# Strassen's seven products for two thirds of the matrix products of a hybrid decoder layer

## The chip, the cores and the metric

The kernel runs on one core of one Trainium2 chip. Its time is the device time of one execution in microseconds (us). The core has a matrix engine (TensorE, PE in the profile, with a unit PEld that loads the stationary operand), a vector engine (DVE), a scalar engine (ACT), GpSimd (POOL) and an engine that here only issues DMAs (SyncE, SP). Each engine works through its own list of instructions in a fixed order; semaphores make one wait for another.

## The reference

A layer for 1024 tokens of width 2048 in float32. One input projection of the normalised input feeds two recurrences: mLSTM with four heads (query, key, value, output gate, z gate, two scalar gates) and HGRN2 with eight heads (query, forget gate, value, output gate). Both are gated, joined, projected back and added to the input; a per-layer input and a second gate follow.

```python
u = rmsnorm(h, norm_w[l])
proj = jnp.einsum('bsd,dc->bsc', u, w_in[l])           # 2048 -> 8200 columns
(ml_q, ml_k, ml_v, ml_o, ml_z, ml_i, ml_f, hg_q, hg_f, hg_i, hg_g) = jnp.split(proj, ...)
h_a = mlstm_chunkwise(q_a, k_a, v_a, i_pre, f_pre)     # q_a, k_a: convolution and silu of ml_q, ml_k
y_a = sigmoid(ml_o) * rmsnorm(h_a) * silu(ml_z)
h_b = hgrn2_chunkwise(q_b, k_b, logf_b, i_b)
y_b = rmsnorm(h_b) * silu(hg_g)
h = h + jnp.einsum('bsc,cd->bsd', concat(y_a, y_b), w_out[l])
e = jnp.einsum('bsr,rd->bsd', p[l], w_pe[l])
gate = sigmoid(jnp.einsum('bsd,de->bse', rmsnorm(h, pe_norm_w[l]), w_pg[l]))
out = rmsnorm(h + gate * e, final_norm_w)
```

## The kernel before

Tokens are handled in two halves of 512. Every large product is a float32 product made of three float32r matmuls: each operand is the sum of a rounded part (hi) and an exact remainder (lo), and `mm3` (lines 241 to 244) issues hi·hi, hi·lo and lo·hi into one accumulator. Making the two parts of an operand is a `split` (lines 113 to 115): a cast on ACT, then a subtraction on DVE.

Weights stream through SBUF in slices of 128 x 1024, each used once per half: `next_piece` (line 140) issues the DMA on SP and the split, three slices ahead of their use (`AHEAD`), into three raw and three split buffers. A block is 256 columns, four slices. `proj_ch` (line 246) puts channels on the output partitions: 96 matmuls of 512 columns into two PSUM banks. `proj_tok` (line 258) puts tokens there: 192 matmuls of 256 columns into four banks. Per half there are 32 blocks: each mLSTM head takes query with key, output gate, values and z; each pair of HGRN2 heads takes values, two blocks of query with forget gate, and the output gate.

The recurrences (`mlstm_unit`, line 342; `hgrn_unit`, line 464) are written behind their own projections. They are chains of small steps that go back and forth between DVE, ACT and PE in chunks of 128 tokens. An mLSTM head multiplies scores (`psc`, `pkt`), then runs over four chunks with a state C (`pn`, `pu`), then a norm (`rh`) and transposes (`pth`). A pair of HGRN2 heads sums elementwise products (`cs_`), doubles block sizes five times (`pl`), updates a state (`hkt`, `hpu`) and reads it out (`hpo`, `hpt`). A tile scheduler decides each engine's order when the kernel is built; it lays these steps between the projection matmuls of later blocks.

The second part (from line 662) does for each half the output projection (`po`, 4 blocks of 512 columns, 8 slices each) with the residual and transposes of the result (`pht`, `hnt`, kept in SBUF), then in `gate_block` the per-layer input (`pe`) and the gate (`pg`), then the final norm. Half 0's output projection is free to start while half 1's recurrences still run.

Matmuls of 512 columns, or as much: 4608 `pj`, 3072 of 256 columns `pt` (1536 as counted in 512), 1536 `po`, 1536 `pg`, 192 `pe`.

Of the kernel before, what the change touches and what calls it, by code (L numbers as in the profile page):

```python
# [869 lines left out]
```

## Time and profile before

| | us |
|---|---|
| median of 3 runs (2429.05 to 2429.24) | 2429.08 |
| span of the profiled execution | 2427.2 |
| PE busy | 2410.4 (99%) |
| PEld busy (beside PE) | 2044.1 (84%) |
| DVE busy | 1166.3 (48%) |
| ACT busy | 767.8 (32%) |
| POOL busy | 66.3 (3%) |
| DMA moved 287.57 MB, mean | 118 GB/s |

The profiled execution's own time is its span and the little around it: the median of the runs is 1.9 us over the span. A group's busy time counts where instructions overlap only once for the engine, but a matmul's own "mean ns" includes the filling of the pipeline, so two neighbours overlap; the step from one start to the next (the pitch) is read from the timeline.

### The profile page before, as it was taken

To read this page: it belongs to the slowest core of one execution; us is meant where nothing else is said; L and a number is where in the kernel's file an instruction comes from. 1 tells how busy PE (TensorE), PEld (TensorE's weight loads), DVE (VectorE), ACT (ScalarE), POOL (GpSimd) and SP (SyncE) were. 2 spreads that over 40 slices of the span, in tenths; PEclk is the share of its full clock that TensorE was granted. 3 is DMA by queue.
4 is the path that set the end of the run, shared out by engine and by line. 5 is a ranking of instruction groups with operands and counts; after the bars stand their busy time and mean duration, and the time that the engine had idled before them with its cause. 6 is when DMAs were issued, how large, how long until landed. Compare 5 with 4: busy or idle time off the path is not lost.

```text
span 2427.2 us, 30855 instructions
## 1 busy us (share of the span) xinstructions
PE 2410.4 (99%) x12700; PEld 2044.1 (84%) x12700; DVE 1166.3 (48%) x1657; ACT 767.8 (32%) x1211; POOL 66.3 (3%) x96
## 2 busy tenths in 40 slices
PE   8999999999999999999999999999999999999998
PEld 7888889888888888888888888888888888888887
DVE  6655344355564847344246364565423444332336
ACT  6433232223222424223222222242322334332225
POOL 0000000000000000000000000000000000000000
PEclk9999999999999999999999999999999999999999
DMA  8433332222222423333332222243444446444336
GB/s 315 136 97 103 94 100 94 91 78 93 79 87 81 156 78 105 96 108 101 94 107 87 87 79 89 78 150 122 135 130 127 132 146 222 135 154 130 117 114 212
DMA packets 93461, 287.57 MB, mean 118 GB/s; under 512 B 10872, under 2 KB 11640, under 8 KB 93320
## 3 DMA queue, kind: packets, MB, share of 16 engines
q1 hardware_dynamic: 88200, 268.82, 35.0%
q0 software_dynamic: 5120, 16.78, 1.8%
q8 instruction: 99, 1.62, 0.3%
q14 instruction: 42, 0.34, 0.0%
HBM read 260.36 MB, written 25.20 MB: 118 GB/s over the span
## 4 chain that ended last, share of the span: by engine, by line
PE 98%; DMA 0%; issue 0%; DVE 0%; ACT 0%; SPq 0%; POOL 0%; POOLq 0%; ACTq 0%; DVEq 0%
PE pj L244 15%; PE pj L243 15%; PE pj L242 15%; PE pg L242 5%; PE pt L242 5%; PE pg L244 5%; PE pt L244 5%; PE pg L243 5%; PE po L242 5%; PE pt L243 5%; PE po L244 5%; PE po L243 5%; PE pl L570 2%; PE pe L242 1%; PE pe L244 1%; PE pe L243 1%
## 5 line engine op out<-in xcount | busy, mean ns | idle before, releaser
L242 PE MATMUL pj<-u,hl 128*128 128x512 f32 x1536 | 608.0, 399 | 5.9 <-ACT hl L114 5.9
L244 PE MATMUL pj<-u,hl 128*128 128x512 f32 x1536 | 611.3, 399 | 0.0
L243 PE MATMUL pj<-u,hl 128*128 128x512 f32 x1536 | 610.8, 398 | 0.2 <-DVE u L230 0.2
L114 ACT CAST hl<-raw 128x1024 fp32r<-128x1024 f32 (+2 forms) x259 | 269.2, 1040 | 863.1 <-PE pj L244 449.1
L115 DVE TENSOR_TENSOR hl<-raw,hl 128x1024 fp32r<-128x1024 f32 (+2 forms) x259 | 313.5, 1211 | 402.4 <-ACT hl L114 402.2
L242 PEld LDWEIGHTS pj<-u,hl 128*128 128x128 f32 x1536 | 289.1, 188 | 72.6 <-ACT hl L114 5.9
L243 PEld LDWEIGHTS pj<-u,hl 128*128 128x128 f32 x1536 | 289.4, 188 | 70.0 <-DVE u L230 1.1
L244 PEld LDWEIGHTS pj<-u,hl 128*128 128x128 f32 x1536 | 289.1, 188 | 66.7 <-issue 0.2
L242 PE MATMUL pt<-hl,u 128*128 128x256 f32 (+1 forms) x1024 | 291.1, 285 | 0.4 <-DVE raw L357 0.4
L244 PE MATMUL pt<-hl,u 128*128 128x256 f32 (+1 forms) x1024 | 290.2, 285 | 0.0
L243 PE MATMUL pt<-hl,u 128*128 128x256 f32 (+1 forms) x1024 | 288.8, 283 | 0.0
L242 PE MATMUL po<-hl_o,ys 128*128 128x512 f32 x512 | 202.1, 395 | 0.0
L244 PE MATMUL po<-hl_o,ys 128*128 128x512 f32 x512 | 200.3, 392 | 0.0
L243 PE MATMUL po<-hl_o,ys 128*128 128x512 f32 x512 | 199.8, 390 | 0.0
L242 PEld LDWEIGHTS pt<-hl,u 128*128 128x128 f32 x1024 | 193.7, 189 | 2.2 <-issue 1.1
L243 PEld LDWEIGHTS pt<-hl,u 128*128 128x128 f32 x1024 | 194.0, 189 | 1.3
L244 PEld LDWEIGHTS pt<-hl,u 128*128 128x128 f32 x1024 | 192.4, 188 | 0.9 <-issue 0.2
L242 PE MATMUL pg<-hl_g,hnt 128*128 128x512 f32 x448 | 177.9, 397 | 0.0
L244 PE MATMUL pg<-hl_g,hnt 128*128 128x512 f32 x448 | 177.9, 397 | 0.0
L243 PE MATMUL pg<-hl_g,hnt 128*128 128x512 f32 x448 | 177.1, 395 | 0.0
L115 DVE TENSOR_TENSOR hl_o<-raw_o,hl_o 128x1024 fp32r<-128x1024 f32 x64 | 78.4, 1225 | 161.9 <-ACT hl_o L114 161.9
L115 DVE TENSOR_TENSOR hl_g<-raw_g,hl_g 128x1024 fp32r<-128x1024 f32 x56 | 68.6, 1225 | 174.5 <-ACT hl_g L114 174.5
(264 smaller groups left out, 2642.9 us busy)
## 6 DMA issues: line engine op xcount, KB each, us to landing
raw<-in_w_blk_dram SPq DMA_DIRECT2D x247, 512.0 KB, 3.9
raw_o<-in_w_out_dram SPq DMA_DIRECT2D x64, 512.0 KB, 3.6
...
yr<-y SPq DMA_DIRECT2D x32, 256.0 KB, 4.0
xr<-in_x_dram SPq DMA_DIRECT2D x32, 256.0 KB, 5.7
h<-ht POOLq DMA_DIRECT2D x32, 256.0 KB, 6.3
hr<-h SPq DMA_DIRECT2D x32, 256.0 KB, 3.6
out_dram<-h SPq DMA_DIRECT2D x32, 256.0 KB, 3.5
```

Source lines behind the costliest of these rows:

```text
L114: nc.scalar.copy(out=dst_hi, in_=src)
L115: nc.vector.tensor_tensor(out=dst_lo, in0=src, in1=dst_hi.bitcast(F32), op=ALU.subtract)
L242: nc.tensor.matmul(ps, lhsT=ah, rhs=bh, start=first, stop=False)
L243: nc.tensor.matmul(ps, lhsT=ah, rhs=bl, start=False, stop=False)
L244: nc.tensor.matmul(ps, lhsT=al, rhs=bh, start=False, stop=last)
L570: nc.tensor.matmul(pl[0:M, c * 64:(c + 1) * 64], lhsT=kf[:, c * P:c * P + M], rhs=qv[:, c * nb:(c + 1) * nb, 1, :], start=True, stop=True)
```

## The change

Seven products in place of eight (Strassen's scheme in Winograd's form). A group takes 512 tokens, 2048 input channels and 1024 columns, cut into quarters: two of 256 tokens, two of 1024 channels, two of 512 columns. Four sums of quarters of the tokens' operand (S1 to S4) and four sums of quarters of the weights stand in the seven products P1 to P7, and the products are added up into the four quarters of the output. It is used for values, all gates of the input projection (5 groups per half), the output projection (2 groups per half) and the second gate of half 0 (2 groups): 16 groups. Query, key and forget-gate projections stay as they were, with channels on partitions; so does the second gate of half 1, with tokens on partitions.

A product has 4 slices of weights of 128 x 1024 and 12 matmuls of 512 columns per slice, so a group has 28 slices and 336 matmuls.

The program is cut into stages that hand over through DRAM.

- Stage a: all of the per-layer input first (192 matmuls `pe`, stored to DRAM), `prep_u` (the norm of the input is now applied to the input, and u is stored to DRAM), then ten groups; gates and values go to DRAM with their nonlinearities applied.
- Stage b: u is loaded and split again; projections of 12 blocks per half, and the recurrences, in the order HGRN2 pair 0, mLSTM head 0, pair 1, head 1 and so on, gates and values loaded from DRAM. The mLSTM scalar gates have 64 matmuls of their own (`pif`).
- Stage c: four groups of the output projection, the residual, transposes stored to DRAM; then half 0's normalised hidden state through DRAM, two groups, and half 1's second gate as before.

All seven operands of the tokens are made in `aprep` before a set of groups: 28 splits and 16 sums of 128 x 512.

```diff
-    upool = ctx.enter_context(tc.tile_pool(name="upool", bufs=17))
-    wpool = ctx.enter_context(tc.tile_pool(name="wpool", bufs=3))
+PRODUCTS = ("P1", "P5", "P2", "P6", "P3", "P7", "P4")
+A_SETS = ("A11", "S1", "A12", "S2", "S4", "S3", "A22")
+    class Gemm:
+            self.up = pool(f"up{tag}", self.st, bufs=28)
+            self.r1p = pool(f"rp{tag}", self.st, bufs=4, side="right")
+            self.hlp = pool(f"hp{tag}", self.st, bufs=3, side="right")
+            self.stp = pool(f"sp{tag}", self.st, bufs=5, side="right")
...
+        def t2(self, name):
+            return self.tp.tile([P, HT], F32, tag="t2", bufs=9, name=name)
...
+                if prod == "P1":
+                    raw = self.r1p.tile([P, 1024], F32, tag="r1", name=f"r1_{n}")
+                    nc.sync.dma_start(out=raw, in_=q["B11"])
+                    self.chain[j] = raw
+                elif prod in ("P5", "P6", "P4"):
+                    raw = self.chain[j]
...
+                        t = self.load(f"s_{n}", b)
+                        nc.vector.tensor_tensor(out=raw, in0=raw, in1=t, op=ALU.add)
+                elif prod == "P7":
+                    raw = self.load(f"s_{n}", q["B12"])
+                    t = self.load(f"t_{n}", q["B22"])
+                    nc.vector.tensor_tensor(out=raw, in0=raw, in1=t, op=ALU.add)
+                else:
+                    raw = self.load(f"s_{n}", q["B21" if prod == "P2" else "B22"])
+            hl = self.hlp.tile([P, 2, 1024], F32R, tag="hl", name=f"hl_{n}")
+            split(hl[:, 0], hl[:, 1], raw)
...
+        for j in range(4):
+            a, b = ld(j + 4, 1), ld(j, 1)
+            c = t2v(f"c{nm}_{j}")
+            nc.vector.tensor_tensor(out=c, in0=a, in1=b, op=ALU.subtract)
+            sc.append(c)
+            put("S1", j, c)
...
+                if pr == "P1":
+                    nc.scalar.copy(out=t("p1", p, "p"), in_=X)
+                elif pr == "P5":
+                    nc.vector.tensor_tensor(out=t("p15", p, "q"), in0=X, in1=tmp["p1", p], op=ALU.add)
+                elif pr == "P2":
+                    done(p, 0, 0, X, None)
+                elif pr == "P6":
+                    nc.vector.tensor_tensor(out=t("u2", p, "r"), in0=X, in1=tmp["p1", p], op=ALU.add)
...
+    for k in range(KT):
+        t = G.t2(f"hk{k}")
+        nc.sync.dma_start(out=t, in_=hT_dram[0][k // 2][k % 2])
+        nc.vector.scalar_tensor_tensor(out=t, in0=t, scalar=vec_sb[:, V_PEN + k:V_PEN + k + 1], in1=rb,
+                                       op0=ALU.mult, op1=ALU.mult)
+        nc.gpsimd.dma_start(out=n_dram[k // 2][k % 2], in_=t)
+    A = aprep(G, "g0", n_dram)
...
+UNITS = [("h", 0), ("m", 0), ("h", 1), ("m", 1), ("h", 2), ("m", 2), ("h", 3), ("m", 3)]
```

The scheduler orders the new program anew. The first place is PE's order at an mLSTM head. Before, at head 1 of half 0, `pn0_1` (chunks read out) and `pu0_1` (state updates) of its recurrence, and `pj0_8`, the projection of a later block:

```order
L243 MATMUL pj0_8_1_1762<-u0_2_179,hl_0_8_0_1600 128x512
L244 MATMUL pj0_8_1_1762<-u0_2_179,hl_0_8_0_1600 128x512
L432 MATMUL pn0_1_1_1699<-C0_1_0_1690,dq0_1_1664 128x257 [waits DVE_49]
L430 MATMUL pn0_1_2_1713<-vt0_1_1531,dq0_1_1664 128x257
L242 MATMUL pj0_8_0_1761<-u0_3_182,hl_0_8_0_1600 128x512
L243 MATMUL pj0_8_0_1761<-u0_3_182,hl_0_8_0_1600 128x512
L244 MATMUL pj0_8_0_1761<-u0_3_182,hl_0_8_0_1600 128x512
L432 MATMUL pn0_1_2_1713<-C0_1_1_1704,dq0_1_1664 128x257 [waits DVE_49]
L435 MATMUL pu0_1_2_1716<-vt0_1_1531,kh0_1_1681 128x257
L242 MATMUL pj0_8_1_1762<-u0_3_182,hl_0_8_0_1600 128x512
L243 MATMUL pj0_8_1_1762<-u0_3_182,hl_0_8_0_1600 128x512
```

Now, for the same head. `pj0_10` is a projection block of the following pair of HGRN2 heads, `pth0_1` the head's last transposes:

```order
L96 MATMUL pj0_10_1_9087<-u0_15_6816,hl_0_10_3_9118 128x512
L642 MATMUL pn0_1_0_8282<-vt0_1_8233,dq0_1_8260 128x257 [waits DMAHW5_49,DVE_49,Activation_49]
L647 MATMUL pu0_1_0_8284<-vt0_1_8233,kh0_1_8277 128x257 [waits DVE_49,Activation_49]
L642 MATMUL pn0_1_1_8295<-vt0_1_8233,dq0_1_8260 128x257 [waits PE_49]
L647 MATMUL pu0_1_1_8298<-vt0_1_8233,kh0_1_8277 128x257 [waits PE_49]
L644 MATMUL pn0_1_1_8295<-C0_1_0_8286,dq0_1_8260 128x257 [waits DVE_49]
L642 MATMUL pn0_1_2_8309<-vt0_1_8233,dq0_1_8260 128x257
L644 MATMUL pn0_1_2_8309<-C0_1_1_8300,dq0_1_8260 128x257 [waits DVE_49]
L647 MATMUL pu0_1_2_8312<-vt0_1_8233,kh0_1_8277 128x257
L642 MATMUL pn0_1_3_8323<-vt0_1_8233,dq0_1_8260 128x257 [waits DVE_49,Activation_49]
L647 MATMUL pu0_1_3_8326<-vt0_1_8233,kh0_1_8277 128x257 [waits DVE_49,Activation_49]
L644 MATMUL pn0_1_3_8323<-C0_1_2_8314,dq0_1_8260 128x257 [waits DVE_49]
L669 MATMUL pth0_1_0_8344<-ident_62,h0_1_8280 128x128 [waits DVE_49]
```

Before, the chunks of the head are laid between projection matmuls; now none stands between the head's first chunk and its last transposes.

The second place is PE's order at the end of the recurrences. Before, near the end of the last pair of half 1 (`hkt1_3`, `hpu1_3`: keys transposed and state update), with the output projection of half 0 (`po0_1`):

```order
L242 MATMUL po0_1_3_13057<-hl_o0_1_0_12937,ys0_1_12675 128x512
L243 MATMUL po0_1_3_13057<-hl_o0_1_0_12937,ys0_1_12675 128x512
L244 MATMUL po0_1_3_13057<-hl_o0_1_0_12937,ys0_1_12675 128x512
L242 MATMUL po0_1_2_13056<-hl_o0_1_1_12966,ys0_2_12680 128x512
L601 MATMUL hpu1_3_0_12579<-hv1_3_12073,hkh1_3_12572 128x128 [waits Activation_49]
L601 MATMUL hpu1_3_0_12579<-hv1_3_12073,hkh1_3_12572 128x128 x3
L597 MATMUL hkt1_3_1_12590<-ident_86,kg1_3_12079 128x128 [waits PE_49]
L597 MATMUL hkt1_3_1_12590<-ident_86,kg1_3_12079 128x128 x3
L243 MATMUL po0_1_2_13056<-hl_o0_1_1_12966,ys0_2_12680 128x512
L244 MATMUL po0_1_2_13056<-hl_o0_1_1_12966,ys0_2_12680 128x512
L242 MATMUL po0_1_3_13057<-hl_o0_1_1_12966,ys0_2_12680 128x512
```

Now, at the end of the last mLSTM head of half 1 (`pn1_3`, `pth1_3`), and the first product of the output projection (`pso00`):

```order
L642 MATMUL pn1_3_3_12771<-vt1_3_12682,dq1_3_12707 128x257
L644 MATMUL pn1_3_3_12771<-C1_3_2_12762,dq1_3_12707 128x257 [waits DVE_49]
L669 MATMUL pth1_3_0_12788<-ident_62,h1_3_12727 128x128 [waits DVE_49,Activation_49]
L669 MATMUL pth1_3_1_12796<-ident_62,h1_3_12727 128x128
L669 MATMUL pth1_3_0_12788<-ident_62,h1_3_12727 128x128 [waits DVE_49]
L669 MATMUL pth1_3_1_12796<-ident_62,h1_3_12727 128x128
L669 MATMUL pth1_3_0_12788<-ident_62,h1_3_12727 128x128 [waits DVE_49]
L669 MATMUL pth1_3_1_12796<-ident_62,h1_3_12727 128x128
L669 MATMUL pth1_3_0_12788<-ident_62,h1_3_12727 128x128 [waits DVE_49]
L669 MATMUL pth1_3_1_12796<-ident_62,h1_3_12727 128x128
L94 MATMUL pso00_X0_1_13016<-hl_o0_0_P1_0_13020,A11o0_0_12837 128x512 [waits Activation_49]
L95 MATMUL pso00_X0_1_13016<-hl_o0_0_P1_0_13020,A11o0_0_12837 128x512 [waits DVE_49]
```

Before, the output projection fills the gaps of the last recurrences; now its first matmul stands behind the last transposes of the last head.

The third place is DVE's order in the output projection. Before, in half 0 (`hl_o`: remainders of weight slices; `hnt`: transposed result; `ht`: residual added):

```order
L115 TENSOR_TENSOR hl_o0_1_6_13175<-raw_o0_1_6_13174,hl_o0_1_6_13175 128x1024 [waits DMAHW6_49,Activation_49]
L115 TENSOR_TENSOR pp0_12748<-praw0_0_12749,pp0_12748 128x512 [waits Activation_49]
L115 TENSOR_TENSOR pp0_12748<-praw0_1_12753,pp0_12748 128x512 [waits Activation_49]
L709 SCALAR_TENSOR_TENSOR hnt0_0_13027<-pht0_0_13022,vec_sb_82,hnt0_0_13027 128x512 [waits Activation_49]
L709 SCALAR_TENSOR_TENSOR hnt0_1_13035<-pht0_1_13030,vec_sb_82,hnt0_1_13035 128x512 [waits Activation_49]
L709 SCALAR_TENSOR_TENSOR hnt0_2_13043<-pht0_2_13038,vec_sb_82,hnt0_2_13043 128x512 [waits DMASW3_49,DMASW2_49,Activation_49]
L709 SCALAR_TENSOR_TENSOR hnt0_3_13051<-pht0_3_13046,vec_sb_82,hnt0_3_13051 128x512 [waits Activation_49]
L115 TENSOR_TENSOR hl_o0_1_7_13204<-raw_o0_1_7_13203,hl_o0_1_7_13204 128x1024 [waits DMAHW7_49,Activation_49]
L115 TENSOR_TENSOR hl_o0_2_0_13233<-raw_o0_2_0_13232,hl_o0_2_0_13233 128x1024 [waits DMAHW0_49,Activation_49]
L115 TENSOR_TENSOR hl_o0_2_1_13262<-raw_o0_2_1_13261,hl_o0_2_1_13262 128x1024 [waits DMAHW1_49,Activation_49]
L696 TENSOR_TENSOR ht0_1_0_13292<-po0_1_0_13054,xr0_1_0_13290 128x512 [waits DMASW6_49,PE_49]
```

Now, in the second group of half 1 (L85: remainders; L151 and L155: sums of weight slices; `u2`, `ht`: products added up):

```order
L155 TENSOR_TENSOR s_o1_1_P7_1_15553<-s_o1_1_P7_1_15553,t_o1_1_P7_1_15555 128x1024 [waits DMAHW3_49,DMAHW2_49,DVE_49]
L85 TENSOR_TENSOR hl_o1_1_P3_3_15518<-s_o1_1_P3_3_15516,hl_o1_1_P3_3_15518 128x1024 [waits DMAHW6_49,Activation_49]
L85 TENSOR_TENSOR hl_o1_1_P7_0_15538<-s_o1_1_P7_0_15533,hl_o1_1_P7_0_15538 128x1024 [waits Activation_49]
L155 TENSOR_TENSOR s_o1_1_P7_2_15573<-s_o1_1_P7_2_15573,t_o1_1_P7_2_15575 128x1024 [waits DMAHW6_49,DMAHW5_49,DVE_49]
L85 TENSOR_TENSOR hl_o1_1_P7_1_15558<-s_o1_1_P7_1_15553,hl_o1_1_P7_1_15558 128x1024 [waits Activation_49]
L269 SCALAR_TENSOR_TENSOR ht1_3_0_15594<-pso11_Z0_1_15263,u2o11_0_15512 128x512 [waits DMASW5_49,PE_49]
L155 TENSOR_TENSOR s_o1_1_P7_3_15627<-s_o1_1_P7_3_15627,t_o1_1_P7_3_15629 128x1024 [waits DMAHW7_49,DMAHW0_49,DVE_49]
L901 TENSOR_TENSOR ht1_3_0_15594<-ht1_3_0_15594,xr1_3_0_15593 128x512 [waits DMAHW4_49,DVE_49]
L85 TENSOR_TENSOR hl_o1_1_P7_2_15578<-s_o1_1_P7_2_15573,hl_o1_1_P7_2_15578 128x1024 [waits Activation_49]
L151 TENSOR_TENSOR r1_o1_1_P1_0_15101<-r1_o1_1_P1_0_15101,s_o1_1_P4_0_15647 128x1024 [waits DMAHW1_49]
L151 TENSOR_TENSOR r1_o1_1_P1_1_15118<-r1_o1_1_P1_1_15118,s_o1_1_P4_1_15665 128x1024 [waits DMAHW2_49]
L85 TENSOR_TENSOR hl_o1_1_P7_3_15632<-s_o1_1_P7_3_15627,hl_o1_1_P7_3_15632 128x1024 [waits DVE_49,Activation_49]
```

Before, each weight slice costs DVE one instruction of 128 x 1024; now a slice of P5, P6, P7 and P4 costs two, and the sums of P5, P6 and P4 go one after the other into one buffer per slice.

## Rows read from the trace of the kernel before

**Rows 1.** The page: busy time, share of the span and instructions of each engine.
```profile
PE 2410.4 (99%) x12700; PEld 2044.1 (84%) x12700; DVE 1166.3 (48%) x1657; ACT 767.8 (32%) x1211; POOL 66.3 (3%) x96
```
**Rows 2.** The page: chain of work that ended last, by engine.
```profile
PE 98%; DMA 0%; issue 0%; DVE 0%; ACT 0%; SPq 0%; POOL 0%; POOLq 0%; ACTq 0%; DVEq 0%
```
**Rows 3.** PE's waits in total: us, times, longest.
```profile
PE pj L242 <- ACT hl L114: 5.9, 1, 5.9
```
**Rows 4.** Timeline of PE at 2000 us: start, us, instruction, tiles (first and 37 later).
```profile
1999.66 0.40 PE L243 MATMUL pg<-hl_g,hnt 128*128 128x512 f32 x1
...
2008.29 0.40 PE L244 MATMUL pg<-hl_g,hnt 128*128 128x512 f32 x1
```
**Rows 5.** Timeline at the end: two 256-column matmuls (eight steps apart), last POOL step.
```profile
2416.75 0.28 PE L242 MATMUL pg<-hl_bg,hnt 128*128 128x256 f32 x1
...
2417.70 0.27 PE L244 MATMUL pg<-hl_bg,hnt 128*128 128x256 f32 x1
...
2420.56 0.54 POOL L120 TENSOR_TENSOR r<-r,neghalf 128x1 f32<-128x1 f32 x1 [5.36 <-DVE r L119]
```
**Rows 6.** Groups on DVE: busy us, mean ns; idle before.
```profile
L115 DVE TENSOR_TENSOR hl<-raw,hl 128x1024 fp32r<-128x1024 f32 x247 | 301.9, 1222 | 390.9 <-ACT hl L114 390.6
L709 DVE SCALAR_TENSOR_TENSOR hnt<-pht,vec_sb,hnt 128x512 fp32r<-128x512 f32 x32 | 21.8, 744 | 18.6 <-ACT hnt L708 18.6
L696 DVE TENSOR_TENSOR ht<-po,xr 128x512 f32<-128x512 f32 x32 | 21.9, 690 | 9.0 <-PE po L244 9.0
L115 DVE TENSOR_TENSOR ys<-yr,ys 128x512 fp32r<-128x512 f32 x32 | 21.3, 687 | 8.4 <-ACT ys L114 8.4
```
**Rows 7.** Windows: length, then busy PE, PEld, DVE, ACT, POOL; granted clock; DMA share; GB/s.
```profile
0.00:62.00 62.00, 55.42 (x248) 44.32 (x249) 39.87 (x77) 38.94 (x67) 1.22 (x5) 1.00 0.86 313
62.00:1600.00 1538.00, 1536.97 (x8723) 1330.27 (x8722) 778.87 (x1141) 450.53 (x720) 36.95 (x44) 1.00 0.30 95
1600.00:2427.00 827.00, 817.98 (x3733) 669.55 (x3731) 347.56 (x441) 278.31 (x424) 28.17 (x47) 1.00 0.46 147
```
**Rows 8.** DMA issues: count, KB each, us to landing.
```profile
yr<-y SPq DMA_DIRECT2D x32, 256.0 KB, 4.0
h<-ht POOLq DMA_DIRECT2D x32, 256.0 KB, 6.3
y<-y POOLq DMA_DIRECT2D x16, 256.0 KB, 2.7
```
**Rows 9.** Timeline of DVE at one mLSTM head: first state, last norm, result.
```profile
201.97 0.43 DVE L438 COPY C<-pu 128x257 f32<-128x257 f32 x1 [0.17 <-PE pu L435]
...
216.73 0.17 DVE L119 TENSOR_SCALAR rh<-ssh 128x4 f32<-128x4 f32 x1 [0.64 <-ACT jkh L449]
...
224.97 1.40 DVE L458 SCALAR_TENSOR_TENSOR y<-pth,vec_sb,gate 128x512 f32<-128x512 f32 x2
```
**Rows 10.** Timeline of PE at that head: two pairs of instructions, each one 257-column product.
```profile
200.90 0.60 PE L430 MATMUL pn<-vt,dq 128*128 128x257 f32 x2
201.34 0.60 PE L435 MATMUL pu<-vt,kh 128*128 128x257 f32 x2
```
**Rows 11.** Timeline of DVE at one pair of HGRN2 heads: first products, result.
```profile
473.25 1.22 DVE L521 TENSOR_TENSOR pd<-hq,kg 128x1024 f32<-128x1024 f32 x1
...
572.30 1.41 DVE L642 SCALAR_TENSOR_TENSOR hy<-hpt,vec_sb,hgate 128x512 f32<-128x512 f32 x2 [0.23 <-PE hpt L640]
```
**Rows 12.** Timeline of PE at the start: first and sixth pair of matmuls.
```profile
5.88 1.22 PE L242 MATMUL pj<-u,hl 128*128 128x512 f32 x2 [5.88 <-ACT hl L114]
...
10.31 0.82 PE L244 MATMUL pj<-u,hl 128*128 128x512 f32 x2
```
**Rows 13.** Windows at the start and after PE's last matmul, columns as in rows 7.
```profile
5.90:10.30 4.40, 4.40 (x10) 3.44 (x11) 2.62 (x9) 1.76 (x5) 0.00 (x0) 1.00 0.87 302
...
2420.00:2422.00 2.00, 0.00 (x0) 0.00 (x0) 1.18 (x4) 0.88 (x3) 0.54 (x1) 0.64 0.00 0
2422.00:2427.00 5.00, 0.00 (x0) 0.00 (x0) 0.28 (x1) 0.47 (x1) 0.00 (x0) 0.50 0.56 210
```

More of the change, by code (lines that the diff above doesn't have):

```diff
@@ new lines, in quarter @@
+    def quarter(o, row, col, X, other):
+        if row == col and other is None:
+            nc.scalar.copy(out=o, in_=X)
+        elif col == 1:
+            nc.vector.scalar_tensor_tensor(out=o, in0=X, scalar=-1.0, in1=other, op0=ALU.mult, op1=ALU.subtract)
+        else:
+            nc.vector.tensor_tensor(out=o, in0=X, in1=other, op=ALU.add)
+    order = [(f"pe_{cb}", "plain", w_pe[cb], False) for cb in range(4)]
+    for half in range(2):
+        order += strassen_order(f"a{half}", w_tok, 5)
@@ new lines, in load_piece @@
+    def load_piece(name):
+        while len(w_tiles) < len(w_order) and (len(w_tiles) < AHEAD or w_order[len(w_tiles) - AHEAD][0] != name):
+            next_piece()
+        return dict(w_tiles[-AHEAD - 4:])[name]
+    wraw = stage.tile([P, HT], F32, tag="xs", name="wifraw")[:, 0:KT * 8].rearrange("p (k c) -> p k c", c=8)
+    nc.sync.dma_start(out=wraw, in_=w_if)
+    wif = wpool.tile([P, KT, 100], F32R, tag="wif", bufs=1, name="wif")
+    nc.vector.memset(wif.bitcast(F32), 0.0)
+    for i in range(2):
+        cs = slice(i * 4, i * 4 + 4)
+        split(wif[:, :, i * 32:i * 32 + 4], wif[:, :, 64 + i * 32:68 + i * 32], wraw[:, :, cs])
@@ new lines, in hybrid_layer, with load_u @@
+    next_piece()
+    def load_u(half):
+        us = []
+        for k in range(KT):
+            if half == 0 and k in (4, 8):
+                next_piece()
+            xt = stage.tile([P, HT], F32, tag="xs", name=f"xt{half}_{k}")
+            nc.sync.dma_start(out=xt, in_=u_dram[half][k // 2][k % 2])
+            u = upool.tile([P, 2, HT], F32R, tag="u", name=f"u{half}_{k}")
+            split(u[:, 0], u[:, 1], xt)
+            us.append(u)
+        return us
+    us = load_u(0)
+    lmask = mix.tile([P, NMASK, 64], U32, name="lmask")
@@ L648, in hybrid_layer @@
     for half in range(2):
[L649 removed]
+        if half == 1:
+            us = load_u(1)
         gc = None
[L651 to L659 removed]
@@ new lines, in hybrid_layer, with done @@
+    for cb, pref in blocks:
+        order += [(f"{pref}g1_{cb}_{pc}", "plain", pg_src(cb, pc), pref == "b" and pc in LATE) for pc in range(8)]
+    G = Gemm("w", order)
+    tl = pool("tl", G.st, bufs=1)
+    psctx = ExitStack()
+    psx = pool("psx2", psctx, bufs=1, space=PS)
+    mx = pool("mx2", psctx, bufs=2, space=PS)
+    i0 = 0
+    sss = []
+    for half in range(2):
+        A = aprep(G, f"o{half}", y_dram[half])
+        ss = small.tile([P, NC, 4], F32, tag="ssx", name=f"ss2_{half}")
+        sss.append(ss)
+        for g in range(2):
+            def done(p, row, col, X, other):
+                t = p + 2 * row
@@ L788, in hybrid_layer @@
[L788 to L793 removed]
+                pt = mx.tile([P, 512], F32, tag="mx", name=f"pht{k}")
+                for j in range(4):
+                    nc.tensor.transpose(pt[:, j * P:(j + 1) * P], ht[:, j * P:(j + 1) * P], ident)
+                hT = G.t2(f"hT{k}")
+                nc.scalar.copy(out=hT, in_=pt)
```

894 lines of the change are left out of this document (513 added, 381 removed).

## The prediction

> **What bounds the kernel now.** I read the page's first section, then the chain that ended last, then PE's waits and a table by stage. PE is busy 2410.4 us of 2427.2 [rows 1], the chain is PE to 98% [rows 2], and PE's largest wait is 5.9 us, before the first matmul [rows 3]. In the long first part PE works 1536.97 of 1538 us while DVE works 778.87, in the second part 817.98 of 827 and 347.56 [rows 7]. So a matmul removed is time gained, as long as PE finds the next one ready, and the reader is to see that so far it always does: DVE is half idle and waits for ACT's casts, which wait for PE [rows 6].
>
> The pitch is 8.63 us over 37 steps, 0.2333 us for a matmul of 512 columns [rows 4], and 0.95 us over 8 steps, 0.119 for 256 columns [rows 5].
>
> **PE's work after.** Before: 4608 + 1536 + 1536 + 192 = 7872 matmuls at 0.2333 are 1837 us, 3072 at 0.119 are 365, and of the 2410 busy that leaves 209 for recurrences and transposes. After: 16 groups of 336 are 5376, the untouched projections 2304, the plain second gate 768, `pe` 192, `pif` 64: 8704 at 0.2333 are 2031 us. The recurrences stay, so 2031 + 210 = 2241 us. The change breaks even if PE idles 2427 - 2241 = 186 us more than nothing; it idles 17 now.
>
> **DVE's work after.** A slice's remainder costs 1.222 us [rows 6], and I take a weight sum (the same operation, type and shape) at the same. Per group: 28 remainders 34.2, 16 sums 19.6, and 14 to 20 additions of products, residuals or gates at 0.69: 62 to 70 us against PE's 336 x 0.2333 = 78.4. So in a plain group DVE has 8 to 16 us in hand; but each slice lasts 2.8 us on PE with three split buffers, and a late remainder stops PE at once. I take 1.5 us for each of the 10 such groups: 15 (nothing to 12 each, the latter if sums and landing never run ahead). Six groups come with `aprep`: 28 remainders at 0.687 and 16 sums at 0.69 are 30 more, 92 to 100 against 78.4. What DVE can do ahead of time is limited by the 28 operand tiles, which the group before still reads, so part shows: 12, 8 and 10 us for the groups of stage a, 10 and 8 for the output projection, 15 for the second gate (that one has sixteen scalings more): 63, between 30 and 120. DVE comes to some 1990 us in all: 16 x 66, 6 x 30, about 583 in stage b by its list of instructions, the rest in the plain gate. That is 88% of PE's new total, and an engine that works in order seldom serves another at 88% without making it wait.
>
> **Where PE has nothing else to do.** Before, the steps of the recurrences stand between projection matmuls in PE's order, so their waiting costs nothing. After, at the mLSTM heads no projection stands between a head's first chunk and its last transposes. That chain took 201.97 to 226.4, 24 us, before [rows 9]; with less between I take 20, and PE's own work in it is 12 products of 257 columns at 0.44 [rows 10], 16 of 128 at no more than 0.119 and five column sums at 0.2333, 8 us. Idle 12 to 13 each at four heads, 22 at the two that also carry the scalar gates: 96. If DVE is far ahead only the steps through C remain, some 5 each: 30. If the full 24 stand, and the scalar gates, 150. 96 lies nearest to the row.
>
> The largest single piece is the end of stage b. Before, the last recurrences are filled with the output projection of half 0. After, everything of stage c stands behind the last transposes, and behind the last projection matmul come the rest of pair 2, head 2, all of pair 3 and head 3. Before, a pair took 473.25 to 573.7, 100 us, with projections between its steps [rows 11]; its DVE work alone is some 45. So 10 + 18 + 45 + 18 = 91 us, in which PE works 36: 55 idle. With the row's full 100, and 24 for each head, it would be 122; with perfect overlap of DVE and PE perhaps 40. I take 55: the row's steps waited mostly for PE's queue, which is now empty.
>
> Through DRAM: a store issued by POOL lands after 2.7 to 6.3 us and a reload by SP takes 4.0 [rows 8], with a step of DVE before and after it. From a to b (values stored, u loaded and split again behind the last evictions) 12; from b to c (y stored, loaded, cast, remainder) 13; before the second gate the norm must be known, then transposes loaded, sixteen scalings at 0.744 [rows 6], stored, loaded again and split, through nine buffers: 12 us of scalings and two passes through DRAM, 27 (20 to 45). On to the plain gate 3. The first matmul waits 5.9 as now [rows 3], and the norm's column and row sums 6 more: 12. The end is 9, as now: after the last matmul comes the same chain [rows 5].
>
> The Trainium skill (DMA: Bandwidth & Descriptors, Anatomy of one DMA) gives a transfer a fixed cost of about 2 us, most of it the receipt that the last byte has landed. By it a store and a reload would cost at least 4 us per hand-over; the trace's landings are longer, so the sum by the rows stands.
>
> **Clock.** The first ten matmuls take 4.43 us from 5.88 to 10.31 [rows 12] where ten at the later pitch take 2.33: 2.1 us lost, though the row for the clock shows 1.00 there [rows 13]. At the end the granted clock falls to 0.50, the lower of the two levels (1.2 GHz), once PE has stood still for some 4 us [rows 13]. So a long idle can cost 2.1 us more when PE resumes; with about a dozen of them, 25 (nothing to 50).
>
> The Trainium skill (TensorE: Matmul & The Clock Gate, The HAM clock gate) says that the throttled clock is the default and only activity releases it. That speaks against a change that brings idle into an engine that had none. The trace agrees in the fall at its end; no row here shows a restart in mid-kernel.
>
> **Sum.** 2241 + 15 + 63 + 96 + 55 + 12 + 13 + 27 + 3 + 12 + 9 = 2546, and 25 for the clock, 2571 as a span. The median stands 1.9 above the span of the profiled execution, so about 2570 us, slower by 6%. With every low end (0, 30, 30, 40, 8, 8, 20, 0, 8, 9, clock 0) it is 2394, with every high end far over 2800; they will not all fall one way.
>
> **Rivals.**
> - PE stays fed. Remainders and chains are ready in time, and only the end of stage b, the start, the end and a few first groups show: 2241 + 40 + 12 + 9 + 30, plus a little at the hand-overs, 2340 to 2400. For it: in plain groups DVE has 8 us in hand, and 186 us of idle are allowed. Against: PE's order itself leaves no projection beside six heads. Chance 0.15.
> - DVE sets the pace in every group, not in six: remainder, sum and product additions share one queue, a sum must wait for its own transfer, and the remainders queued behind it on DVE wait with it. Each of the ten plain groups then takes about 90 in place of 78, 120 more: about 2690. For it: P5, P6 and P4 add one after the other into one buffer per slice, so a sum can't be made early. Against: 62 to 70 is below 78. Chance 0.2. It decides from 78 us of DVE per group.
> - Transfers. A group reads 32 slices of 512 KB, 16.8 MB in 78 us, 215 GB/s, where the mean of the second part is 147. Against: 313 GB/s went in the first 62 us [rows 7], with PE busy 55 of them. If landing goes from 4 to 8 us, five raw buffers at 2.8 us still cover it except in P7, which takes two: 4 products' worth of waits, some 60 us in all, 2630. Chance 0.05.
>
> **How the numbers follow.** Forecast near 2570 (its own range 2450 to 2660) 0.6, and the rivals 0.15, 0.2 and 0.05. A measurement of this kernel tells 0.2%, 5 us, from no change. Faster takes the first rival, nearly all, 0.15; same a sliver between it and the low end of the forecast, 0.03; slower 0.82. The range for 8 in 10 is 2400 to 2720.
>
> **What would show it.** PE's busy time near 2241 and its waits near 300 us, by line: before the output projection's first product one wait of some 50 or more in pieces, at each head about 13, before the first group of each set about 10; DVE near 1990 busy. Wrong would be: waits of PE under 186 us in all; or PE waiting for `hl` in every slice of every group (then it is the second rival); or DVE's sums at another duration than 1.222.

## The result: 12.5% slower, outside the range

The changed kernel takes 2732.52 us (median of 4 runs, 2731.57 to 2737.05) against 2429.07 before: a ratio of 1.1253, 95% interval 1.1237 to 1.1269. The direction was forecast (slower, 0.82), the size was not: 2570 was predicted, and the range ended at 2720. The profiled execution has a span of 2730.6 us.

The page's first section of the changed kernel, to be held against [rows 1]:

```profile
PE 2364.3 (87%) x10462; PEld 1885.2 (69%) x10462; DVE 1868.0 (68%) x2486; ACT 1079.7 (40%) x1603; POOL 207.1 (8%) x333
```

PE does 2238 instructions less than before and is busy 46 us less, where 170 less were expected. It stands still for 366 us (2730.6 - 2364.3) where it stood still for 17. DVE's load is 6% under its forecast (1990 predicted, 1868 measured).

The chain that ended last is PE no more [rows 2]:

```profile
PE 39%; DMA 21%; DVE 21%; issue 14%; ACT 3%; POOL 1%; SPq 0%; DVEq 0%; ACTq 0%; POOLq 0%
```

Windows over the stages of the changed kernel, columns as in [rows 7]: the ten groups of stage a; stage b; its end behind the last projection matmul; the output projection; the hand-over to the second gate; that gate's two groups; the plain gate.

```profile
82.00:969.00 887.00, 807.67 (x3370) 636.45 (x3368) 682.00 (x720) 371.74 (x423) 45.03 (x81) 0.97 0.68 231
969.00:1794.00 825.00, 739.69 (x3632) 606.16 (x3632) 498.18 (x880) 271.05 (x499) 30.99 (x38) 0.93 0.31 100
1794.00:1905.00 111.00, 61.46 (x300) 50.09 (x298) 62.14 (x140) 33.87 (x94) 9.97 (x12) 0.67 0.26 88
1905.00:2305.00 400.00, 350.20 (x1456) 271.41 (x1456) 302.56 (x338) 183.00 (x257) 56.53 (x85) 0.93 0.79 268
2305.00:2351.00 46.00, 6.42 (x19) 3.36 (x18) 23.38 (x33) 7.51 (x15) 17.72 (x29) 0.56 0.89 306
2351.00:2531.00 180.00, 165.41 (x672) 128.86 (x672) 154.55 (x178) 93.34 (x129) 7.42 (x14) 0.96 0.83 279
2531.00:2720.00 189.00, 180.60 (x816) 147.52 (x816) 102.82 (x137) 76.42 (x118) 12.62 (x23) 0.98 0.72 242
```

The reader is to subtract PE's busy time from each length: 79, 85, 50, 50, 40, 15 and 8 us. The sixth and seventh lines are the same product, each for one half of the tokens: two seven-product groups (672 matmuls) take 180 us and 46 before them, the plain gate (768) 189. The clock's column was 1.00 in every stage before [rows 7]; it is now under 1.00 in all seven stretches, lowest in the hand-over (0.56) and at the end of stage b (0.67).

PE's waits in total in the changed kernel, the largest; before, one line of 5.9 us led this view [rows 3]:

```profile
PE pht L907 <- DVE ht L901: 38.3, 12, 7.3
PE pth L669 <- DVE h L664: 32.5, 8, 4.4
PE psg_X L94 <- ACT A11g L84: 26.2, 1, 26.2
PE psa_Z L94 <- DVE g L269: 24.5, 1, 24.5
PE psa_Z L95 <- DVE hl_a_P L85: 18.8, 9, 6.4
PE gcol L566 <- ACT stk L563: 18.5, 1, 18.5
PE pc L293 <- DVE acc L290: 16.6, 1, 16.6
PE psa_Y L95 <- DVE hl_a_P L85: 15.5, 11, 2.7
...
PE psa_X L95 <- DVE hl_a_P L85: 10.4, 9, 2.5
...
PE pso_Y L95 <- DVE hl_o_P L85: 6.8, 6, 4.0
...
PE pso_Z L95 <- DVE hl_o_P L85: 4.9, 8, 1.4
PE psg_Y L94 <- ACT hl_g_P L84: 4.1, 3, 2.7
```

Weight slices (`hl_a`, `hl_o`, `hl_g`) come as many small waits, 78 us in the 17 lines that name them; the large lines are transposes, hand-overs and heads of the recurrences. In the fourth, a single place in a group, DVE itself was waiting; it is shown here, in DVE's timeline and then PE's:

```profile
338.61 1.22 DVE L151 TENSOR_TENSOR r_a_P<-r_a_P,s_a_P 128x1024 f32<-128x1024 f32 x1
339.75 1.22 DVE L85 TENSOR_TENSOR hl_a_P<-r_a_P,hl_a_P 128x1024 fp32r<-128x1024 f32 x1
352.20 5.45 DVE L297 SCALAR_TENSOR_TENSOR xt<-xt,vec_sb,rbsx 128x512 f32<-128x512 f32 x8 [11.23 <-DMA xt<-in_xT_dram]
358.09 1.47 DVE L363 TENSOR_TENSOR g<-psa_X,s 128x512 f32<-128x512 f32 x2 [0.45 <-ACT s L362]
359.48 1.28 DVE L269 SCALAR_TENSOR_TENSOR g<-psa_Z,u2a 128x512 f32<-128x512 f32 x2
```

```profile
360.31 0.76 PE L94 MATMUL psa_Z<-hl_a_P,A22a 128*128 128x512 f32 x1 [24.50 <-DVE g L269]
```

DVE stands 11.2 us in front of a scaling (`xt`, of half 1's input) whose operand hasn't landed; behind it in its queue are the evictions of the current group, and PE needs the bank that the last of them frees. On SP's side the loads of `xt` were queued behind weight slices:

```profile
334.28 4.11 SPq L142 DMA_DIRECT2D r_a_P<-in_w_tok_dram  x2
339.86 0.33 SPq L122 DMA_DIRECT2D s_a_P<-in_w_tok_dram  x1
340.99 0.33 SPq L142 DMA_DIRECT2D r_a_P<-in_w_tok_dram  x1
341.41 10.38 SPq L406 DMA_DIRECT2D xt<-in_xT_dram  x8
```

### The profile page after: what moved, and what is told of

Its sections match the earlier page's. It is cut to its first block, busy times and chain, and to the rows that moved or that the text cites. A ratio compares the mean times of both kernels' runs of the same rounds, so it can differ in the third digit from the quotient of the medians.

```text
span 2730.6 us, 29545 instructions
## 1 busy us (share of the span) xinstructions
PE 2364.3 (87%) x10462; PEld 1885.2 (69%) x10462; DVE 1868.0 (68%) x2486; ACT 1079.7 (40%) x1603; POOL 207.1 (8%) x333
## 4 chain that ended last, share of the span: by engine, by line
PE 39%; DMA 21%; DVE 21%; issue 14%; ACT 3%; POOL 1%; SPq 0%; DVEq 0%; ACTq 0%; POOLq 0%
DMA s_a_P<-in_w_tok_dram 5%; PE pj L94 5%; PE pj L95 5%; PE pj L96 5%; DVE hl_a_P L85 4%; DMA t_a_P<-in_w_tok_dram 3%; DVE r_a_P L151 2%; PE pl L776 2%; PE pg L94 2%; DMA r_a_P<-in_w_tok_dram 2%; PE pg L95 2%; DMA t_o_P<-in_w_out_dram 2%; PE pg L96 2%; DVE hl_o_P L85 2%; DMA s_o_P<-in_w_out_dram 1%
## 5 line engine op out<-in xcount | busy, mean ns | idle before, releaser
L94 PE MATMUL pj<-u,hl 128*128 128x512 f32 x768 | 308.6, 405 | 16.9 <-ACT u L84 11.5
L95 PE MATMUL pj<-u,hl 128*128 128x512 f32 x768 | 307.1, 400 | 0.1
L96 PE MATMUL pj<-u,hl 128*128 128x512 f32 x768 | 306.6, 400 | 0.0
L84 ACT CAST hl_a_P<-r_a_P 128x1024 fp32r<-128x1024 f32 x160 | 167.8, 1050 | 222.5 <-PE psa_X L96 77.9
L85 DVE TENSOR_TENSOR hl_a_P<-r_a_P,hl_a_P 128x1024 fp32r<-128x1024 f32 x160 | 193.8, 1220 | 74.2 <-ACT hl_a_P L84 74.2
L84 ACT CAST hl_a_P<-s_a_P 128x1024 fp32r<-128x1024 f32 x120 | 126.2, 1051 | 194.1 <-PE psa_Z L96 90.2
L85 DVE TENSOR_TENSOR hl<-raw,hl 128x1024 fp32r<-128x1024 f32 x96 | 116.7, 1221 | 116.1 <-ACT hl L84 115.9
L84 ACT CAST hl<-raw 128x1024 fp32r<-128x1024 f32 x96 | 100.2, 1050 | 226.3 <-PE pj L96 219.6
L151 DVE TENSOR_TENSOR r_a_P<-r_a_P,s_a_P 128x1024 f32<-128x1024 f32 x120 | 146.4, 1221 | 56.2 <-DMA s_a_P<-in_w_tok_dram 55.4
L94 PEld LDWEIGHTS pj<-u,hl 128*128 128x128 f32 x768 | 148.4, 194 | 51.4 <-ACT u L84 12.8
L95 PEld LDWEIGHTS pj<-u,hl 128*128 128x128 f32 x768 | 148.3, 193 | 31.7 <-DVE u L85 1.5
L96 PEld LDWEIGHTS pj<-u,hl 128*128 128x128 f32 x768 | 148.1, 193 | 30.8
L85 DVE TENSOR_TENSOR hl_a_P<-s_a_P,hl_a_P 128x1024 fp32r<-128x1024 f32 x120 | 145.2, 1219 | 28.0 <-ACT hl_a_P L84 28.0
L85 DVE TENSOR_TENSOR hl_o_P<-r_o_P,hl_o_P 128x1024 fp32r<-128x1024 f32 x64 | 77.9, 1220 | 32.1 <-ACT hl_o_P L84 23.6
L94 PE MATMUL pg<-hl_g,hn 128*128 128x512 f32 x192 | 76.9, 401 | 8.4 <-ACT hn L974 8.4
L94 PE MATMUL psa_Z<-hl_a_P,A22a 128*128 128x512 f32 x160 | 59.2, 408 | 26.4 <-DVE g L269 24.5
L95 PE MATMUL pg<-hl_g,hn 128*128 128x512 f32 x192 | 76.7, 399 | 0.0
L96 PE MATMUL pg<-hl_g,hn 128*128 128x512 f32 x192 | 74.3, 396 | 0.0
```

Of the source, the lines that this page charges most:

```text
L84: nc.scalar.copy(out=dst_hi, in_=src)
L85: nc.vector.tensor_tensor(out=dst_lo, in0=src, in1=dst_hi.bitcast(F32), op=ALU.subtract)
L94: nc.tensor.matmul(ps, lhsT=ah, rhs=bh, start=first, stop=False, skip_group_check=more)
L95: nc.tensor.matmul(ps, lhsT=ah, rhs=bl, start=False, stop=False, skip_group_check=more)
L96: nc.tensor.matmul(ps, lhsT=al, rhs=bh, start=False, stop=last, skip_group_check=more)
L151: nc.vector.tensor_tensor(out=raw, in0=raw, in1=t, op=ALU.add)
```

## The experiments

Each is compared with the changed kernel's 2732.5 us; the ratio is to the kernel before, with its 95% interval.

**Weight sums left out.**

```diff
-                        nc.vector.tensor_tensor(out=raw, in0=raw, in1=t, op=ALU.add)
+                        pass
...
-                    nc.vector.tensor_tensor(out=raw, in0=raw, in1=t, op=ALU.add)
```

> Leaves the sixteen weight sums of every group out (P5, P6, P4 and P7 use one quarter as it is; all transfers stay), 313 us less work for DVE. Theory A, waits: PE loses time at single places where one DVE instruction stands behind others or behind a transfer, and the clock falls there; the sums matter little outside the groups with operand preparation: 30 to 80 us faster than the changed kernel (2732), plain groups from 83-85 to about 81 us. Theory B, DVE's amount of work sets the pace of the groups: the 206 us that the sixteen groups take over their matmuls go nearly all, about 150 us faster. Theory C, transfers set it: within 20 us of 2732.

Measured: 2737.02 us, 1.1266 (1.125 to 1.1283). 281 us of DVE's work are gone and nothing is gained: theory B falls, A's 30 to 80 us are missed too, and the time is that of theory C. But the waits are not the same ones. Those for weight slices fall from 78 to 38 us, and others grow by as much. PE's and DVE's waits in this run:

```profile
PE pht L906 <- DVE ht L900: 63.7, 10, 10.4
PE psa_Z L94 <- DVE g L268: 37.5, 1, 37.5
...
PE psa_X L94 <- ACT hl_a_P L84: 21.0, 7, 5.4
```

```profile
DVE ht L900 <- DMA xr<-in_x_dram: 68.5, 14, 12.8
```

DVE now waits 68.5 us for the residual's loads, where in the changed kernel it was 23.5:

```profile
DVE ht L901 <- DMA xr<-in_x_dram: 23.5, 9, 4.3
```

**Transposes left out.**

```diff
-                pt = mx.tile([P, 512], F32, tag="mx", name=f"pht{k}")
-                for j in range(4):
-                    nc.tensor.transpose(pt[:, j * P:(j + 1) * P], ht[:, j * P:(j + 1) * P], ident)
-                hT = G.t2(f"hT{k}")
-                nc.scalar.copy(out=hT, in_=pt)
+                hT = ht
```

> Leaves the transposes of the output projection's result out (the result is stored as it is). PE waited 38 us at these transposes for DVE's residual sums. Theory A, waits in PE's own order: these 38 us, the 15 us of transposes and a few us of low clock go, 45 to 60 us faster than 2732. Theory B, the same lateness would show at the next weight slice: only the 15 us go.

Measured: 2682.28 us, 1.1038 (1.1022 to 1.1055): 50 us faster, as theory A has it.

**Transposes later.** They are put on a list and issued before the third slice of the next product.

```diff
+                if j == 2:
+                    for f in late:
+                        f()
```

> The same transposes issued half a product later, nothing left out. Theory A: most of the 38 us of waits go, since the residual sums have some 6 us more: 20 to 35 us faster than 2732. Theory B: the waits move to other instructions, within 8 us of 2732.

Measured: 2695.76 us, 1.111 (1.1065 to 1.1154): 37 us faster, with nothing left out, a little over theory A. PE's wait at the transposes falls from 38.6 to 19.5 us.

**Scaling pass left out.**

```diff
-    A = aprep(G, "g0", n_dram)
+    A = aprep(G, "g0", hT_dram[0])
```

> Leaves the scaling of half 0's hidden state out (norm weight and 1/rms), so that the second gate's operands are made from the stored transposes at once, without the second pass through DRAM. The gap before the gate's first product took 40.9 us. Theory A, latency of the passes: the gap falls to about 14 us as between the two halves of the output projection, 25 to 32 us faster. Theory B, DVE's work: the sixteen scalings at 0.745 go, 12 us.

Measured: 2715.27 us, 1.1171 (1.1154 to 1.1188): 17 us faster, between the theories. From the last product's first transposes to the gate's first matmul it is now 14 us in place of 41, but the two groups and the wait behind them took 193 us in place of 188; the other 5 us stay open.

**Filler at the low clock.**

```diff
+    def fill(ps, n):
+        for _ in range(n):
+            nc.tensor.matmul(ps.rearrange("p (c t) -> p c t", t=P), lhsT=ones_r, rhs=fillt, start=True, stop=True)
```

> Adds matmuls of no use (512 columns, a constant operand) into PSUM tiles before their first use, where PE stands still in the recurrences: 16, 20 and 8 at each mLSTM head, and some in the last pair of heads, about 520 in all, 121 us of PE work, to keep PE's clock up without shortening any chain. Theory A1, the clock costs by itself: in the stage of the recurrences (929 us, 59 of them matmuls at the low clock) the low clock goes, and where the filler lies inside the waits 20 to 50 us are gained there. Theory A2, only the waits count and the low clock lies where PE waits anyway: nothing is gained, and filler that outlasts a wait costs up to 50 us.

Measured: 2765.86 us, 1.1386 (1.1365 to 1.1407): 33 us slower, within A2. Windows of stage b, changed kernel and then this run:

```profile
975.00:1905.00 930.00, 800.96 (x3929) 656.26 (x3929) 556.36 (x1004) 301.98 (x588) 39.88 (x48) 0.90 0.31 98
```

```profile
973.00:1933.00 960.00, 880.73 (x4386) 726.42 (x4384) 561.98 (x1019) 303.94 (x592) 40.94 (x50) 0.95 0.30 96
```

The filler brings the mean clock from 0.90 to 0.95. Its 456 matmuls are some 106 us at the full pitch; PE stands still 50 us less (129 to 79), its busy time grows by only 80, so some 26 us come from the clock and from fewer stops, and 30 are lost on balance. So the clock does cost something here, as A1 says, but not what it takes to keep it up.

**The second gate of half 0 plain.** The two groups, the scaling pass and their operands make way for `gate0`, a copy of the plain product for half 0.

```diff
-    order += strassen_order("g0", w_pg, 2)
+        order += [(f"g0_{cb}_{pc}", "plain", pg_src(cb, pc), False) for pc in range(8)]
```

> Undoes one part: the second gate of half 0 as eight plain products with tokens on partitions, like half 1's, instead of seven. In the changed kernel's trace the gap and the two groups took 41 + 93 + 95 = 229 us for 672 matmuls, half 1's plain gate 181 for 768. Theory A: 25 to 50 us faster than 2732, though 96 matmuls (22 us) more are done. Theory of the change (fewer matmuls are less time): up to 22 us slower.

Measured: 2713.35 us, 1.1169 (1.1152 to 1.1186): 19 us faster with 96 matmuls more. Here the seven products lose, together with the scaling pass and the second trip through DRAM that they need; by less than expected.

**Spread scaling.**

```diff
-            if half == 0 and g == 1:
+            if half == 0 and g < 4:
...
+              scale_u(1, xs, rx1, range(4 * g, 4 * g + 4), g)
```

> Spreads the scaling of half 1's input (sixteen steps behind group 1 of half 0) over four groups, four steps each; the same work in all. In the changed kernel eight of these steps stood in DVE's queue for 11 us for their transfer, and behind them the eviction for which PE waited 24.9 us. Theory A, standing behind a waiting instruction: 15 to 28 us faster than 2732. Theory B, amount of work: within 8 us.

Measured: 2706.57 us, 1.1143 (1.1123 to 1.1164): 26 us faster, and the wait of 24.5 us has left the list.

**Early loads of the residual.**

```diff
+            if early is not None and rc:
+                for p in range(2):
+                    early(p, *rc)
```

> Issues the loads of the residual at the start of the product instead of its end; nothing else. In the changed kernel PE waited 38 us at the transposes, DVE 23.5 us for these loads, which stand on SP's queue behind weight slices that wait for a buffer. Theory A, late transfers: 15 to 30 us faster than 2732. Rival: DVE's queue (sums and remainders ahead of the addition) makes the residual late, then within 8 us.

Measured: 2719.55 us, 1.1184 (1.1162 to 1.1207): 13 us faster, a little under theory A. DVE's wait for these loads falls from 23.5 to 2.0 us, PE's at the transposes from 38.3 to 19.0. The other half would be DVE's own queue, the rival; this run doesn't show it.

**Eight products in the same stages.**

```diff
-PRODUCTS = ("P1", "P5", "P2", "P6", "P3", "P7", "P4")
+PRODUCTS = ("B11", "B21", "B12", "B22")
...
+                            mm3(banks[t], As[j][:, 0, kk, ts], As[j][:, 1, kk, ts], hl[kk][0], hl[kk][1],
```

> Eight plain products in place of seven in all sixteen groups, in the same stages, with the same passes through DRAM, the same recurrences: 768 matmuls more (179 us at 0.2333), no sums of weights or of token operands, half the weight transfers. Theory A, the seven products' saving is taken back inside the groups by waits that they themselves bring: within 40 us of 2732. Theory of the change, the saving is there and the staging alone costs: about 2732 + 179 = 2911 us.

Measured: 2745.91 us, 1.13 (1.1284 to 1.1317). Theory A: of 179 us of matmuls the seven products keep 13. The window of its ten groups of stage a and that of its stage b up to the last projection:

```profile
76.00:1000.00 924.00, 902.08 (x3850) 725.58 (x3850) 261.02 (x264) 241.99 (x288) 45.24 (x83) 0.99 0.40 127
1000.00:1823.00 823.00, 740.23 (x3629) 606.18 (x3630) 497.17 (x871) 271.36 (x500) 30.49 (x37) 0.93 0.32 100
```

Two things are to be read here. The groups stand still for 22 us instead of 79, at 127 GB/s instead of 231. And stage b is the same to 2 us: what is lost there belongs to the stages, not to the seven products. This run does before's matmuls in the changed kernel's stages and is 316 us slower than before, so the staging, with its passes through DRAM and its preparation of operands, loses about that by itself.

**Another order of the recurrences.**

```diff
-UNITS = [("h", 0), ("m", 0), ("h", 1), ("m", 1), ("h", 2), ("m", 2), ("h", 3), ("m", 3)]
+UNITS = [("h", 0), ("h", 1), ("h", 2), ("h", 3), ("m", 0), ("m", 1), ("m", 2), ("m", 3)]
```

> Another order of the recurrences in stage b: the four pairs of HGRN2 heads first, then the four mLSTM heads. After the last projection then come some mLSTM heads' chains instead of a pair's and two heads'. Theory A, an exposed tail of 110 us with 36 us of PE work: the pair's 45 us go from the tail, but mLSTM chains (24 us each) then stand behind projections of 22 us and cover each other badly: 10 to 40 us faster. Rival, the tail was bound by DVE's total work in stage b: within 8 us.

Measured: 2720.71 us, 1.1198 (1.1179 to 1.1217): 12 us faster, at theory A's low end.

**Sums of P6 and P4 by the DMA.**

```diff
-ACCUM = False
+ACCUM = True
```

> Lets the DMA add two of the four sums of weights per group (P6 and P4), issued by GpSimd, instead of DVE: 128 additions of 1.22 us less on DVE. Theory A and the run without sums: DVE's work isn't what PE waits for, so nothing is gained (within 15 us), and accumulating transfers issued behind GpSimd's waiting stores can make slices late: up to 100 us slower. Theory B: 40 us faster.

Measured: 2731.6 us, 1.1254 (1.1228 to 1.128): no change, though DVE's busy time falls from 1868 to 1730. The bytes are the same.

**Second summands not loaded, sums made.**

```diff
-                        t = self.load(f"s_{n}", b)
-                        nc.vector.tensor_tensor(out=raw, in0=raw, in1=t, op=ALU.add)
+                        nc.vector.tensor_tensor(out=raw, in0=raw, in1=raw, op=ALU.add)
```

(and likewise for P7; of 32 loads of weights per group 16 stay)

> All sums of weights are made, but each adds a slice to itself: the sixteen loads of the second summands of each group are left out (12 or 16 of 28 to 32 slices stay; DVE's work is the same). Theory C, transfers: the groups' waits (169 us) and their low clock fall towards those of the run with eight products (45 us), 80 to 150 us faster than 2732. Theory B, DVE's amount of work or its order: within 30 us.

Measured: 2644.15 us, 1.0887 (1.0871 to 1.0903): 88 us faster, within theory C. Page of this run, and the window of stage a:

```profile
PE 2344.0 (89%) x10462; PEld 1879.8 (71%) x10462; DVE 1869.5 (71%) x2486; ACT 1074.7 (41%) x1603; POOL 207.2 (8%) x333
```

```profile
82.00:890.00 808.00, 767.20 (x3255) 612.72 (x3256) 669.90 (x705) 363.16 (x417) 43.03 (x77) 0.98 0.44 147
```

DVE works as long as in the changed kernel; the transfers move 147 GB/s instead of 231.

**Neither loaded nor summed.** Both edits together.

```diff
-                        t = self.load(f"s_{n}", b)
-                        nc.vector.tensor_tensor(out=raw, in0=raw, in1=t, op=ALU.add)
+                        pass
```

> Neither second summands loaded nor sums made: a group then has the transfers and DVE work of twelve slices fewer, and PE's work as it is. Theory C: about as the run with the sums made (within 30 us of it), since DVE wasn't the limit. Theory B plus C, either is enough to hold PE up: 50 us or more faster than the run with sums, though leaving out the sums alone gained nothing.

Measured: 2575.65 us, 1.0607 (1.059 to 1.0625). The four runs make a table:

| | second summands loaded | not loaded |
|---|---|---|
| sums made | 2732.5 | 2644.2 |
| not made | 2737.0 | 2575.7 |

With the loads in place the sums cost nothing in the total, and once the loads are gone they cost 69 us. Of the theories the last comes nearest, but not to the letter, since the loads alone are worth 88 us. PE's waits in the four runs (us: all lines that wait for `hl_a`, `hl_o` or `hl_g`; the transposes `pht`; the one wait of `psa_Z` for an eviction `g`) show why the first column is flat:

| | weight slices | `pht` | `psa_Z` for `g` |
|---|---|---|---|
| changed kernel | 78 | 39 | 24.5 |
| no sums | 38 | 70 | 37.5 |
| no second loads | 40 | 19 | 22.9 |
| neither | 8 | 8 | 16.3 |

At the weight slices sums and loads count alike, about 40 us each. Without the sums these 40 us come back at two places where DVE stands behind a load, the residual and half 1's input. Why those loads are later in that run isn't shown. Nor is it separated whether the second loads hurt by their bytes, by their places in SP's queue or by the buffers that they hold, for leaving them out takes away all three; half of them in GpSimd's queue, with the same bytes, changed nothing (the run with the sums by the DMA).

**The mendings together.** Late transposes, early loads, spread scaling, plain second gate: the edits shown above in one kernel.

```diff
-            strassen_group(G, i0, f"o{half}{g}", A, psx, done)
+            strassen_group(G, i0, f"o{half}{g}", A, psx, done, early)
...
+                G.late.append(turn)
```

> Late transposes, early loads of the residual, the spread scaling and the plain second gate together, all results kept. Theory A: the single gains (36, 13, 26, 19 us) add but for the overlap of the first two: 2732 - 75 = 2657, between 2640 and 2680 us; still slower than the kernel before, since the recurrences' waits stay.

Measured: 2636.38 us, 1.0848 (1.0824 to 1.0873): 96 us faster than the changed kernel, 4 us more than theory A's best. The single gains (37, 13, 26 and 19 us) add in full; the overlap that was expected of the first two didn't show. With the other order of the recurrences as well:

```diff
+UNITS = [("h", 0), ("h", 1), ("h", 2), ("h", 3), ("m", 0), ("m", 1), ("m", 2), ("m", 3)]
```

> The four mendings of the combined run with the recurrences in the order of the run that did the pairs of heads first; all results kept. If the gains add: 2636 - 12 = 2624 us, between 2610 and 2640; still 8% slower than the kernel before.

Measured: 2621.95 us, 1.0791 (1.0772 to 1.081). This is the best version of the seven products that was run with nothing left out, and it is no match for the kernel before. A version that beats both wasn't found; seven products inside before's own loops weren't tried, nor more buffers for the loads.

## Why the prediction was wrong

The sum had ten terms of standing still, 305 us in all, and 25 us for the clock, on 2241 us of matmuls. Set against the windows (the length less PE's busy time) and the waits:

| term | predicted | measured |
|---|---|---|
| start | 12 | 27 (8.6 `pe`, 16.6 `pc`, 2.2 `rbx`) |
| sixteen groups | 78 | 144 (79 + 50 + 15) |
| a to b, heads in stage b | 108 | 85 |
| end of stage b, b to c | 68 | 50 |
| to the second gate | 27 | 40 (26 for operands, 13 at the transposes) |
| plain gate and end | 12 | 19 |
| sum | 305 | 365 |
| PE busy over 2241 | 25 | 123 |

The span is 160 us over the forecast (2730.6 against 2571). 98 of them are in the last row and 61 in the waits, so two steps failed, and the clock's is the larger.

**The clock was mis-sized.** 2.1 us for each of a dozen restarts came from the first matmuls [rows 12], 25 in all. PE's busy time is 123 us over the forecast with the same matmuls. Behind the waits of 6 to 26 us that end in matmuls of 512 columns the pitch is 0.427 us, as here behind the hand-over to the second gate, until it falls to 0.233:

```profile
2352.39 0.63 PE L94 MATMUL psg_X<-hl_g_P,A11g 128*128 128x512 f32 x1
2352.82 0.63 PE L95 MATMUL psg_X<-hl_g_P,A11g 128*128 128x512 f32 x1
...
2355.26 0.40 PE L95 MATMUL psg_X<-hl_g_P,A11g 128*128 128x512 f32 x1
2355.49 0.40 PE L96 MATMUL psg_X<-hl_g_P,A11g 128*128 128x512 f32 x1
```

From 2351.37 to 2355.03 nine matmuls took 3.66 us, 1.6 more than at the full pitch, in line with the row. The count was wrong. The trace has 31 stretches at the lower level (granted 0.50, 1.2 GHz), and the last line of a table of windows laid over just these stretches gives their length and the busy time in them:

```profile
sum 389.61, PE 198.78 PEld 145.88 DVE 258.03 ACT 114.05 POOL 65.66; mean PE 6.41 PEld 4.71 DVE 8.32 ACT 3.68 POOL 2.12
```

PE is busy there for 199 us. At the ratio of the two pitches the same work would take 109 at the upper level, an estimate that takes the ratio for all matmuls: 90 of the 123 us are then the clock, and the other 33 aren't explained (the end of the last matmul before each wait counts as busy and is part of them). 116 of the 199 us lie in stage b with its end, where the recurrences are: the sum had priced restarts, not whole chains of short matmuls at the lower level. With eight products in the same stages PE is busy at the lower level for 161 us, 118 of them in stage b: most of this cost belongs to the stages, not to the seven products. The filler puts what can be had back in stage b at some 26 us. (The fall in [rows 13] was read a little off: the last matmul ends at 2417.97, and a mean of 0.64 from 2420 to 2422 puts the fall at 2420.6, 2.6 us behind it and not some 4. The sum doesn't hang on that.)

The Trainium skill (TensorE: Matmul & The Clock Gate, The HAM clock gate) has the throttled state as the default that activity releases; this run agrees, with granted clocks of 0.56 to 0.98 in stages that wait and 1.00 in all stages before.

**The other failed step is the one on the groups.** It argued from amounts: 62 to 70 us of DVE in 78 of PE, "so in a plain group DVE has 8 to 16 us in hand", and let the waits follow from that, 15 us for ten groups and 63 for six. The amounts were right: a weight sum measured 1.221 us on DVE, and 85 us of a plain group hold 63.6 of DVE. The waits for weight slices came out at 78 us, as forecast, but with some luck: DVE's sums are only half of them, and the loads of the second summands, a rival with a chance of 0.05, are the other half, as the table of the four runs shows. The rival was dismissed because 313 GB/s had gone in the first 62 us [rows 7]. That row says what the engines can move, not when a load lands that stands in SP's queue behind others. The median landing, which counts from the issue, went from 3.9 us before to 5.1 in stage a and 6.5 in the output projection:

```profile
s_a_P<-in_w_tok_dram SPq DMA_DIRECT2D x240, 512.0 KB, 5.1
raw<-in_w_ch_dram SPq DMA_DIRECT2D x96, 512.0 KB, 3.8
s_o_P<-in_w_out_dram SPq DMA_DIRECT2D x96, 512.0 KB, 6.5
```

With eight products in the same stages it was 3.9 us in stage a and 4.8 in the output projection.

Most of what makes 144 of 78 was put at nothing. The transposes of the output projection's result wait 38.6 us (13 of them within the hand-over to the second gate): their matmuls are issued in PE's queue right behind their product and wait for a residual that DVE adds late; a step was moved next to a long chain, and what stands behind it was not asked. And 24.5 us is the one eviction behind DVE's scaling of half 1's input, which waited for its load. Late transposes (37 us), early loads (13) and the spread scaling (26) show both.

**What held, and what was too high.** The worth of a matmul left out: with eight products PE is busy 94 us longer in stage a for 480 matmuls more, 112 at the full pitch; a part of the 18 between is the clock (24 us busy at the lower level with seven products, 8 with eight). The hand-overs: 11.5 us for u where 12 were forecast from a to b, 10.1 of 13 from b to c, 27 of 27 before the second gate without the transposes. Too high were the recurrences: 55 us of waits were predicted for the end of stage b, where 39 are measured, and 96 for the mLSTM heads, where `pth`, `gcol` and `pn` come to 53 (the sums `cs_` of the HGRN2 heads, which the sum left out, are 15 more). So errors of both signs met in the waits. The cause on the largest scale was seen: the staging takes away the cover under which recurrences and hand-overs cost nothing; by the run with eight products this alone is 316 us, more than the whole loss.

## What to carry to other kernels

A scheme that saves matmuls pays with transfers and with steps between them. Work both out per slice against the time that a slice lasts on PE, and ask for each load which queue issues it, behind what, and which engine stands in front of it, before adding up busy times: DVE at 68% was still late in many places. Where a kernel is bound by one engine at 99%, a change that cuts it into stages must first name what runs beside every chain in each stage, and price the chain's own matmuls at the lower clock as well as its waits.
